# A hybrid attention/recurrence block on one core: PSUM as two allocations of four adjacent banks, a block's four sums added by one instruction, the second norm's factor applied once

## The chip, the cores and the metric

The kernel runs on one core of one Trainium2 chip. The metric is device time in microseconds (us) of one execution, from its start to its end; lower is better. Engines are named as in the profile: PE is TensorE (matmul), PEld its weight loads, DVE is VectorE, ACT is ScalarE, POOL is GpSimd, SP issues most of the DMAs.

## The reference, cut to what matters

One decoder layer over 256 positions of 2048 features, all in float32:

```python
a    = rmsnorm(h, norm_mix_pre)
proj = a @ w_in                       # 2048 x 17408: q, k, v of 3 attention groups, 4 parts of the recurrence, 2 gates
...                                   # rotary, three dilated windows of attention, merged by softmax denominators
...                                   # HGRN2 gated linear recurrence, per-head norm, output gate
y    = sigmoid(gate_a) * (attn @ w_attn_branch) + sigmoid(gate_r) * (r_out @ w_hgrn_branch)
h    = h + rmsnorm(y @ w_mix_out, norm_mix_post)
a    = rmsnorm(h, norm_ffn_pre)
gt, up = split(a @ w_ffn_gate_up)     # 2048 x (5632 + 5632)
ff   = (silu(gt) * up) @ w_ffn_down   # 5632 x 2048
h    = h + rmsnorm(ff, norm_ffn_post)
```

## The kernel before, in words

Every weight matrix is streamed once. `load` brings a piece of 512 KB into a `raw` buffer (SP's queue); `split` or `split_wide` makes of it a high part (ACT, a copy to the reduced-precision type fp32r) and a low part (DVE, the difference); `multiply` or `multiply_wide` then issues three products per tile (high by high, high by low, low by high) on PE, by the helper `mm` (L135). Work is a list of *blocks*, each of some *steps*. The order on every engine is the order in which the Python program issues instructions (`manual_schedule`); the split of a step stands two steps ahead of its matmuls (`AHEAD = 2`).

There are three kinds of block:

- **W blocks** (32 of them, four steps each): 256 columns of the weights are the stationary operand's columns, so results come out transposed, in two banks of PSUM. They make the recurrence's and the attention's projections. When one is done, `both_halves` evacuates it: for each of the two banks ACT copies one half (L237), then DVE adds the other half to it (L239).
- **N blocks** (12): 512 columns, two banks, one for each half of the positions. The two branch products, the output gate of the recurrence and the first piece of the feed-forward network's gate and up products are such blocks.
- **Wide blocks** (22, class `Wide`): 1024 columns, four result banks, keyed (side, group). Some of their steps save a product by a seven-product scheme, which needs four more banks, "p1", "p5", "p6" and "p7"; `gather` combines these into four pieces of SBUF (`b.rest`) after the last such step, and the block's evacuation (`evac_kept`, `evac_mix`, `evac_ffn`, `evac_down`) adds each result bank to its piece, bank by bank (for the feed-forward network L1327).

PSUM has eight banks of 2 KB per partition. Before, each bank is a tile of its own, drawn from two pools of four: `acc_bank()` and `aux()`. N and W blocks take two `acc` banks each, so two blocks alternate between two pairs. Wide blocks put their four results in one pool and the products "p1" to "p7" in the other, and swap (`flip`). Small work (transposes, attention, recurrence) takes `aux` banks; `turn_act` (L1295 and L1296) transposes a feed-forward result into two banks, which ACT copies out; `turn_side` (in the passage from the first half of the layer to the second) takes `acc` banks.

The evacuation of a block is a generator in the queue `evacs`. The main loop advances it by one `yield` after the matmuls of each step, so that the reads of a finished W or N block are issued **after** the matmuls of the next block's first step, which write the other pair of banks. Small work stands in the queues `lanes` and `turns`, advanced in the same place.

Of the kernel before, what the change touches and what calls it, by code (L numbers as in the profile page):

```python
# [19 lines left out]
P = 128  # L20
# [73 lines left out]
def tile_hybrid_block(ctx: ExitStack, tc: tile.TileContext, t, out):  # L94
# [7 lines left out]
    accp = ctx.enter_context(tc.tile_pool(name="accp", bufs=4, space=PSUM))  # L102
    auxp = ctx.enter_context(tc.tile_pool(name="auxp", bufs=4, space=PSUM))
# [14 lines left out]

    def aux():
# [8 lines left out]
    def eslot(s="e"):  # L128
        return p3(s, F32, 512, 6, "e")
# [103 lines left out]
    def both_halves(ev, i):  # L233
        def go(banks):
            s = ptile("sum").rearrange("p (h t) -> p h t", h=2)
            for n, ps in enumerate(banks):
                nc.scalar.activation(s[:, n, :], ps[:, S:], AF.Copy)  # L237
            for n, ps in enumerate(banks):
                nc.vector.tensor_add(s[:, n, :], ps[:, :S], s[:, n, :])  # L239
            yield from ev(i, s)  # L240
        return go
# [117 lines left out]

    def multiply_wide(st, sides=(0, 1), groups=(0, 1)):  # L360
        b, i = st.block, st.i
        m, by7 = b.order[i]

        def bank(key):

            if key not in b.bank:
                b.bank[key] = aux() if b.flip == (type(key) is not tuple) else acc_bank()
            return b.bank[key]

        def prod(key, x, w, j, last=False):  # L370
            ps = bank(key)
# [24 lines left out]
        prod((1, 1), act_of(1, 1), t, 3)  # L396

    def gather(b):

        e = {k: p3("e", F32, 512, 6) for k in ((0, 1), (1, 1), (0, 0), (1, 0))}  # L400
        x = b.bank
        nc.scalar.activation(e[0, 1], x["p1"], AF.Copy)
        nc.vector.tensor_add(e[1, 1], x["p6"], e[0, 1])
        nc.vector.tensor_add(e[0, 0], x["p5"], e[1, 1])
# [34 lines left out]
    class Split:  # L439
# [41 lines left out]
        def turned(self, src, n0, n):  # L481

            for i in range(n):
                ps = aux()
                for kk in range(2):
                    for b in range(2):
                        at = kk * S + b * P
                        c = (2 * i + kk) * P
                        nc.tensor.transpose(ps[:, at : at + P], src[:, b, c : c + P], ident)  # L489
                yield  # L490
                self.put(n0 + i, ps.rearrange("p (k t) -> p k t", k=2))

    def transpose_in(src, gcol, dst, c, apart=False):

        ps = []
        for k in (2 * c, 2 * c + 1):
            if apart or not ps:
                bank = aux()
            ps.append(bank[:, :S] if apart else bank[:, (k % 2) * S : (k % 2 + 1) * S])
# [10 lines left out]
        def low(kk):  # L510
            k = 2 * c + kk
            nc.vector.scalar_tensor_tensor(
                out=dst(k)[1], in0=ps[kk], scalar=gcol[:, k : k + 1],
                in1=dst.f32(k), op0=OP.mult, op1=OP.subtract,
            )

        if apart:
            return high, low
        high(0), high(1), low(0), low(1)

    def row_broadcast(dst, rc):
# [9 lines left out]
        nc.scalar.activation(dst, ps[:, :S], AF.Copy)  # L531

# [56 lines left out]
    def opening():  # L589
# [14 lines left out]
        nc.vector.tensor_copy(colg[:, 16:48], ps[:, :32])  # L604
        l0, l1 = colg[:, 32:40], colg[:, 40:48]
# [23 lines left out]
    def keep_warm(n):  # L629

        ps = aux()
        for _ in range(n):
            mm(ps, warm[:, :P], warm, True, True)

    def start():
# [3 lines left out]
        nc.vector.tensor_copy(colg[:, :16], ps[:, :16])  # L639
        high, low = transpose_in(xt, colg, xT, 0, True)  # L640
# [29 lines left out]
    def evac_kept(key, fn):  # L670
        def go(b):
            dst, at = keep(key, 1024), [(0, 0), (0, 1), (1, 0), (1, 1)]
            for k in at:
                nc.vector.tensor_add(b.rest[k], b.bank[k], b.rest[k])
            for s, g in at:
                e = b.rest[s, g]
                nc.scalar.activation(e, e, fn, scale=r1c[:, s : s + 1])
                nc.gpsimd.dma_start(dst[:, s, g * 512 : (g + 1) * 512], e)
                if (s, g) == (0, 1):
                    yield  # L680
            yield
# [64 lines left out]
    def evac_g(half):  # L746
        def go(banks):
# [4 lines left out]
            for i, ps in enumerate(banks):  # L752
                nc.scalar.activation(s[i], ps, AF.Sigmoid, scale=r1c[:, i : i + 1])
                nc.scalar.activation(dst[:, i, :], ps, AF.Copy, scale=r1c[:, i : i + 1])
            for _ in range(1 if half == 0 else 4):
                yield
# [46 lines left out]
    def attention(pair, hh):  # L803
# [4 lines left out]
        for par in range(2):  # L808
# [15 lines left out]
            nc.scalar.activation(p, p, AF.Exp, scale=-1.0, bias=m[:, 0:1], accum_out=m[:, 1:2])  # L824
            yield
# [10 lines left out]
            nc.scalar.activation(pt, ps, AF.Copy)  # L836
            yield
# [9 lines left out]
        nc.vector.tensor_sub(lo, o[:, :S], attnT[0].f32(head))  # L847
        done.append(head)
# [3 lines left out]
    def recurrence(half):  # L852
# [28 lines left out]
        def over_features(x, place):  # L881
# [5 lines left out]
            def go():  # L887
# [10 lines left out]
                for ps, there in zip(banks, place):  # L898
                    yield
                    there(ps)  # L900

# [40 lines left out]
        def products(lev, w):  # L942

            ps = aux()
            if w < 64:
# [7 lines left out]
                put(lev, w)(ps)  # L953
            elif w == 64:
# [7 lines left out]
                )  # L962
            else:
# [5 lines left out]
                nc.scalar.activation(a2[0], ps, AF.Copy)  # L969

# [48 lines left out]
        for i in range(2):  # L1019
            for h in range(4):  # L1020
# [4 lines left out]
                )  # L1025
            yield
        yield
        for j in range(2):
# [7 lines left out]
            recT[0].put(2 * half + j, ps.rearrange("p (h t) -> p h t", h=2), True)  # L1036
            if j == 1:
# [8 lines left out]
    def evac_rec_branch(j):  # L1046
        def go(banks):
            part[j] = hslot("part")
            for i in range(2):
                nc.vector.tensor_mul(part[j][:, i, :], banks[i], gates["r", j][:, i, :])  # L1050
                yield
        return go

    def evac_attn_branch(j):
        def go(banks):
# [3 lines left out]
            for i in range(2):  # L1059
                nc.vector.tensor_mul(g[:, i, :], banks[i], g[:, i, :])  # L1060
            yield
# [42 lines left out]
    def mix_sum(j, i, b):  # L1104
        e = b.rest[i, j % 2]
        nc.vector.tensor_add(e, b.bank[i, j % 2], e)

    def mix_square(j, i, b):
        sq = zss[0][:, 4 * i + j : 4 * i + j + 1]
        nc.scalar.activation(ptile("junk"), b.rest[i, j % 2], AF.Square, accum_out=sq)  # L1110

    def mix_gain(j, i, b):
        if j not in zg:
            zg[j] = sided(rslot("zg"))
        nc.vector.tensor_mul(
            zg[j][:, i, :], b.rest[i, j % 2],
# [3 lines left out]
    def evac_mix(b):  # L1120
        at = [(j, i) for i in range(2) for j in range(2)]
        for j, i in at:
            mix_sum(j, i, b)
# [28 lines left out]
    def turn_side(c, i):  # L1152
# [12 lines left out]
        def low():  # L1165
            for k, x in at:
# [3 lines left out]
                )  # L1170
        return high, low
# [114 lines left out]
    def turn_act(u, b):  # L1286
# [3 lines left out]
        for i in range(2):  # L1290
# [7 lines left out]
            )  # L1298

    def evac_first_gate(banks):  # L1300
        g = gate_t[0] = [eslot("g") for _ in range(2)]
        src = banks
        if "r2" not in ready:
            for i in range(2):
                nc.scalar.activation(g[i], banks[i], AF.Copy)
                yield
            src = g
            while "r2" not in ready:
                yield
        for i in range(2):  # L1310
            nc.scalar.activation(g[i], src[i], AF.Silu, scale=r2c[:, i : i + 1])
            yield

    def evac_first_up(banks):
        u = [eslot("u") for _ in range(2)]
        for i in range(2):
            nc.vector.scalar_tensor_tensor(
                out=u[i], in0=banks[i], scalar=r2c[:, i : i + 1], in1=gate_t[0][i],
                op0=OP.mult, op1=OP.mult,
            )  # L1320
        turns.append(u)
        yield

    def evac_ffn(b):
        e, x = b.rest, b.bank
        for key in ((0, 0), (0, 1), (1, 0), (1, 1)):
            nc.vector.tensor_add(e[key], x[key], e[key])  # L1327
            s, g = key
            if g == 0:
                nc.scalar.activation(e[key], e[key], AF.Silu, scale=r2c[:, s : s + 1])  # L1330
        yield
        for s in range(2):
            nc.vector.scalar_tensor_tensor(
                out=e[s, 1], in0=e[s, 1], scalar=r2c[:, s : s + 1], in1=e[s, 0],
                op0=OP.mult, op1=OP.mult,
            )
        turns.append([e[0, 1], e[1, 1]])
# [33 lines left out]
    def down_sum(j, i, b):  # L1371

        f = b.rest[i, j % 2]
        nc.vector.tensor_add(f, b.bank[i, j % 2], f)  # L1374

    def down_square(j, i, b):
        sq, r2 = fss[0][:, 4 * i + j : 4 * i + j + 1], r2c[:, i : i + 1]
        nc.scalar.activation(ptile("junk"), b.rest[i, j % 2], AF.Square, scale=r2, accum_out=sq)  # L1378

    def down_gain(j, i, b):  # L1380
        if i == 0:
            fz[j] = p3("fz", F32, 1024, 4, "so").rearrange("p (b c) -> p b c", b=2)
        nc.vector.scalar_tensor_tensor(
            out=fz[j][:, i, :], in0=b.rest[i, j % 2], scalar=r2c[:, i : i + 1],
# [4 lines left out]
    def evac_down(b):  # L1389
        parts = [(j, i) for i in range(2) for j in range(2)]  # L1390
        for j, i in parts:
            down_sum(j, i, b)
# [224 lines left out]
```

## Time and profile before

| | |
|---|---|
| median of 3 timed runs | 1701.61 us (1701.57 to 1703.21) |
| the profiled execution, first to last instruction | 1699.6 us |
| PE busy | 1689.1 us, 99% |
| DVE busy | 1423.5 us, 84% |
| ACT busy | 908.5 us, 53% |
| POOL busy | 40.5 us, 2% |
| granted TensorE clock, mean | 0.998 |

The profiled execution is one run beside the timed ones; its span is 2.0 us under their median, which is what lies before the first and after the last instruction and the difference from run to run. A group row of the profile reads: line, engine, operation, tiles out and in, shapes, how often, then busy us and mean ns of one. A timeline row reads: start us, us, engine, line, operation, tiles, how often. In the last column of either stands the idle time before it and who ended it. Line numbers of the profile are those of the kernel before; in the changed kernel `mm` is L157, the two reads of a W block are L259 and L261, and `turn_act` is L1347 and L1348.

### The profile page before, as it was taken

How to read it: one execution, taken by the hardware profiler on the slowest of the kernel's cores; microseconds unless marked ns; L12 is line 12 of the kernel's file. 1: busy time of each engine (PE TensorE's matmuls, PEld its weight loads, DVE VectorE, ACT ScalarE, POOL GpSimd, SP SyncE). 2: the span in 40 equal slices, each digit the busy share in tenths (PEclk: the TensorE clock that was granted, in tenths of full speed). 3: DMA queues.
4: the chain of work that ended last, by engine and by line, in shares of the span. 5: the costliest groups of instructions: out<-in, count | busy, mean ns of one | idle time of the engine just before them, and what ended most of it. 6: DMA issues, size and time to landing. Idle time of an engine off the chain costs nothing.

```text
span 1699.6 us, 21507 instructions
## 1 busy us (share of the span) xinstructions
PE 1689.1 (99%) x8265; PEld 1420.0 (84%) x8265; DVE 1423.5 (84%) x1604; ACT 908.5 (53%) x1023; POOL 40.5 (2%) x72
## 2 busy tenths in 40 slices
PE   9999999999999999999999999999999999999997
PEld 7888888888888888888888888888888888888886
DVE  6998888886887987776668889888888888898988
ACT  6655555554535434544445575555555555565663
POOL 0000000001000000000000000000000000000000
PEclk9999999999999999999999999999999999999999
DMA  8666666667546555565457646555555555656653
GB/s 288 220 231 232 232 232 233 228 229 258 180 149 196 188 174 175 173 216 168 154 179 249 237 147 223 198 198 198 198 198 198 198 198 198 221 195 212 200 198 114
DMA packets 206614, 344.77 MB, mean 203 GB/s; under 512 B 10960, under 2 KB 77568, under 8 KB 206512
## 3 DMA queue, kind: packets, MB, share of 16 engines
q1 hardware_dynamic: 198208, 317.89, 55.7%
q0 software_dynamic: 5680, 19.60, 3.3%
q10 hardware_dynamic: 2624, 5.92, 1.0%
q8 instruction: 64, 1.05, 0.2%
q14 instruction: 38, 0.31, 0.1%
HBM read 331.83 MB, written 11.53 MB: 202 GB/s over the span
## 4 chain that ended last, share of the span: by engine, by line
PE 98%; DVE 1%; ACT 0%; issue 0%; DVEq 0%; ACTq 0%
PE acc L135 61%; PE aux L135 35%; PE aux L833 0%; PE aux L501 0%; PE acc L1295 0%; DVE fz L1422 0%; PE aux L1295 0%; PE aux L489 0%; ACT junk L1378 0%; DVE e L1374 0%; DVE w L302 0%; DVE wl L338 0%; PE aux L1033 0%; PE acc L1158 0%; DVE g L758 0%
## 5 line engine op out<-in xcount | busy, mean ns | idle before, releaser
L338 DVE TENSOR_TENSOR wl<-raw,w 128x2048 fp32r<-128x2048 f32 x134 | 306.8, 2289 | 92.3 <-ACT w L336 90.9
L135 PE MATMUL acc<-xT,w 128*128 128x256 f32 (+1 forms) x2048 | 369.8, 339 | 0.0
L135 PEld LDWEIGHTS acc<-xT,w 128*128 128x128 f32 x2048 | 312.0, 188 | 43.8
L302 DVE TENSOR_TENSOR w<-raw,w 128x1024 fp32r<-128x1024 f32 (+1 forms) x191 | 232.5, 1218 | 136.0 <-ACT w L301 135.1
L336 ACT ACTIVATE w<-raw 128x2048 fp32r<-128x2048 f32 x134 | 256.1, 1911 | 149.3 <-PE aux L135 62.6
L301 ACT ACTIVATE w<-raw 128x1024 fp32r<-128x1024 f32 (+1 forms) x191 | 200.9, 1053 | 230.2 <-PE acc L135 187.8
L135 PE MATMUL acc<-w,hT 128*128 128x512 f32 x598 | 175.5, 390 | 0.0
L347 ACT ACTIVATE w<-sum 128x1024 fp32r<-128x1024 f32 x70 | 74.4, 1063 | 186.5 <-DVE sum L342 186.5
L355 DVE TENSOR_TENSOR wl<-sum,w 128x1024 fp32r<-128x1024 f32 (+1 forms) x128 | 168.8, 1321 | 0.0
L135 PE MATMUL acc<-w,xT 128*128 128x512 f32 x536 | 155.1, 392 | 0.0
L135 PE MATMUL aux<-w,hT 128*128 128x512 f32 x430 | 135.7, 389 | 0.0
L135 PEld LDWEIGHTS acc<-w,hT 128*128 128x128 f32 x598 | 111.7, 188 | 23.2 <-DVE w L302 0.2
L357 DVE TENSOR_TENSOR dl<-raw,dh 128x1536 fp32r<-128x1536 f32 x70 | 123.0, 1758 | 8.8 <-ACT dh L353 7.2
L135 PEld LDWEIGHTS acc<-w,xT 128*128 128x128 f32 x536 | 99.9, 188 | 20.9 <-DVE w L302 0.3
L135 PE MATMUL aux<-w,xT 128*128 128x512 f32 x344 | 108.5, 389 | 0.0
L353 ACT ACTIVATE dh<-raw 128x1536 fp32r<-128x1536 f32 x70 | 103.1, 1473 | 0.0
L135 PEld LDWEIGHTS aux<-w,hT 128*128 128x128 f32 x430 | 80.7, 188 | 16.8
L135 PE MATMUL acc<-wl,hT 128*128 128x512 f32 x227 | 86.9, 390 | 0.0
L350 ACT ACTIVATE w<-sum 128x1024 fp32r<-128x1024 f32 x70 | 74.4, 1062 | 21.8 <-DVE sum L349 21.8
L342 DVE TENSOR_TENSOR sum<-raw 128x1024 f32<-128x1024 f32 x70 | 85.2, 1217 | 0.0
L135 PE MATMUL aux<-wl,hT 128*128 128x512 f32 x215 | 83.6, 389 | 0.0
L135 PE MATMUL aux<-w,a 128*128 128x512 f32 x268 | 83.6, 389 | 0.0
(293 smaller groups left out, 2776.8 us busy)
## 6 DMA issues: line engine op xcount, KB each, us to landing
raw<-in_w_in SPq DMA_DIRECT2D x271, 512.0 KB, 4.6
raw<-in_w_ffn_gate_up SPq DMA_DIRECT2D x176, 512.0 KB, 4.4
raw<-in_w_ffn_down SPq DMA_DIRECT2D x88, 512.0 KB, 4.8
raw<-in_w_mix_out SPq DMA_DIRECT2D x32, 512.0 KB, 5.3
kept<-e POOLq DMA_DIRECT2D x32, 256.0 KB, 4.2
raw<-in_w_hgrn_branch SPq DMA_DIRECT2D x16, 512.0 KB, 4.9
raw<-in_w_attn_branch SPq DMA_DIRECT2D x16, 512.0 KB, 4.5
v<-kept POOLq DMA_DIRECT2D x8, 512.0 KB, 5.7
```

What stands on the lines that cost most here:

```text
L135: nc.tensor.matmul(ps, lhsT, rhs, start=start, stop=stop, skip_group_check=True)
L301: nc.scalar.activation(wh[:, k], raw[:, k], AF.Copy)
L302: nc.vector.tensor_sub(wl[:, k], raw[:, k], wh[:, k].bitcast(F32))
L336: nc.scalar.activation(hi, raw, AF.Copy)
L338: nc.vector.tensor_sub(lo, raw, hi.bitcast(F32))
L342: nc.vector.tensor_sub(s[:, :1024].rearrange("p (a c) -> p a c", a=2), raw[:, 512:1536].rearrange("p (a c) -> p a c", a=2), raw[:, None, : ...
L347: nc.scalar.activation(hi[:, :1024], s[:, :1024], AF.Copy)
L350: nc.scalar.activation(hi[:, 1024:], s[:, 1024:], AF.Copy)
L353: nc.scalar.activation(dhi, d, AF.Copy)
L355: nc.vector.tensor_sub(lo[:, x], s[:, x], hi[:, x].bitcast(F32))
L357: nc.vector.tensor_sub(dlo, d, dhi.bitcast(F32))
```

## The change

1. PSUM is now two tiles, `acc` and `aux`, of four adjacent banks each, which live from the beginning to the end. `bank_of` hands out a view of one bank from a list of idle ones and `free` gives it back; both are bookkeeping in Python and issue nothing.
2. A wide block takes its four result banks at once, in order (`all_four`), so that `add_up` adds all four banks to the four pieces by one DVE instruction of 128x2048. The four pieces are one tile (`four_e`) with one buffer instead of six small ones.
3. `gather`'s last two additions, which both add "p7", are one instruction.
4. In the feed-forward network the second norm's factor `r2c` was applied to the gate and to the up product, and again after the down product; now it is left out at the up product, and the two products per block are one instruction of 128x1024.
5. The kept results are written by two DMAs of 512 KB per block instead of four of 256 KB.

```diff
-    accp = ctx.enter_context(tc.tile_pool(name="accp", bufs=4, space=PSUM))
-    auxp = ctx.enter_context(tc.tile_pool(name="auxp", bufs=4, space=PSUM))
+    psum = ctx.enter_context(tc.tile_pool(name="psum", bufs=1, space=PSUM))
...
+    fours = {n: psum.tile([P, 4, 512], F32, name=n) for n in ("acc", "aux")}
+    idle = {n: deque(range(4)) for n in fours}
+    held = {}
+    def bank_of(n):
+        i = idle[n].popleft()
+        ps = fours[n][:, i, :]
+        held[id(ps)] = (n, i, ps)
+        return ps
...
     def aux():
-        return auxp.tile([P, 512], F32, tag="aux", name=nm("aux"))
+        return bank_of("aux")
     def acc_bank():
-        return accp.tile([P, 512], F32, tag="acc", name=nm("acc"))
+        return bank_of("acc")
...
-        nc.vector.tensor_add(e[1, 0], x["p7"], e[0, 0])
-        nc.vector.tensor_add(e[1, 1], x["p7"], e[1, 1])
+        nc.vector.tensor_add(
+            e[:, 2:], x["p7"][:, None, :].to_broadcast([P, 2, 512]), e[:, 0:4:3]
+        )
...
+    def add_up(b):
+        nc.vector.tensor_add(b.rest, out_of(b), b.rest)
+        free_out(b)
...
     def evac_ffn(b):
-        for key in ((0, 0), (0, 1), (1, 0), (1, 1)):
-            nc.vector.tensor_add(e[key], x[key], e[key])
...
-            nc.vector.scalar_tensor_tensor(
-                out=e[s, 1], in0=e[s, 1], scalar=r2c[:, s : s + 1], in1=e[s, 0],
-                op0=OP.mult, op1=OP.mult,
-            )
+        add_up(b)
...
+        nc.vector.tensor_mul(e[:, 1:4:2], e[:, 1:4:2], e[:, 0:4:2])
```

The instructions on PE stay, 8031 matmuls in nearly the same order. What each waits for moves. A row below is a line, an instruction with its tiles, its shape, and in brackets the engines' semaphores that it waits for.

**PE, at the border of the first two W blocks**, the end of the second block's first step and the beginning of its second step (`xT` is the activations, `w` the split weights). Before:

```order
L135 MATMUL acc_3128<-xT_113,w_3081 128x512
L135 MATMUL acc_3128<-xT_113,w_3081 128x256 x2
L135 MATMUL acc_3128<-xT_113,w_3081 128x512
L135 MATMUL acc_3127<-xT_114,w_3102 128x512 [waits Activation_49]
L135 MATMUL acc_3127<-xT_114,w_3102 128x256 [waits DVE_49]
L135 MATMUL acc_3127<-xT_114,w_3102 128x256
```

Of the change, at the same place:

```order
L157 MATMUL acc<-xT_112,w_2908 128x512
L157 MATMUL acc<-xT_112,w_2908 128x256 x2
L157 MATMUL acc<-xT_112,w_2908 128x512
L157 MATMUL acc<-xT_113,w_2929 128x512 [waits DVE_49,Activation_49]
L157 MATMUL acc<-xT_113,w_2929 128x256 x2
```

Before, the second step's first matmul waits for ACT's high part of its weights and the second for DVE's low part. In the change the first also waits for DVE, and the counts in the built program are those of the second DVE add (L261) and the second ACT copy (L259) of the *first* block, which read the other pair of banks.

**ACT, at the same border**: the splits of the steps ahead, and between them the two copies out of the first block's banks. Before:

```order
L301 ACTIVATE w_3102<-raw_2911 128x1024 [waits DMAHW0_49,DVE_49,PE_49]
L301 ACTIVATE w_3122<-raw_2941 128x1024 [waits DMAHW1_49,DVE_49,PE_49]
L237 ACTIVATE sum_3145<-acc_3043 128x256
L237 ACTIVATE sum_3145<-acc_3044 128x256
L301 ACTIVATE w_3152<-raw_2941 128x1024 [waits DMAHW2_49,DVE_49,PE_49]
```

Of the change:

```order
L324 ACTIVATE w_2929<-raw_2751 128x1024 [waits DMAHW0_49,DVE_49,PE_49]
L324 ACTIVATE w_2949<-raw_2781 128x1024 [waits DMAHW1_49,DVE_49,PE_49]
L259 ACTIVATE sum_2970<-acc 128x256 [waits PE_49]
L259 ACTIVATE sum_2970<-acc 128x256
L324 ACTIVATE w_2977<-raw_2781 128x1024 [waits DMAHW2_49,DVE_49]
```

The order is the same; the copy now waits for PE, and its count in the built program is that of the last matmul of the second block's first step, which writes a bank that the copy does not read.

**PE, at `turn_act` of the first wide block of the feed-forward network**: two banks, four transposes each. Before:

```order
L135 MATMUL aux_8589<-w_8528,hT_8009 128x512
L1295 MATMUL acc_8628<-ident,u_8547 128x128 [waits DVE_49]
L1295 MATMUL acc_8628<-ident,u_8548 128x128 [waits DVE_49]
L1295 MATMUL acc_8628<-ident,u_8547 128x128
L1295 MATMUL acc_8628<-ident,u_8548 128x128
L1295 MATMUL acc_8634<-ident,u_8547 128x128
```

Of the change:

```order
L157 MATMUL aux<-w_8157,hT_7654 128x512
L1347 MATMUL acc<-ident,e_8033 128x128 [waits DVE_49]
L1347 MATMUL acc<-ident,e_8033 128x128 x3
L1347 MATMUL acc<-ident,e_8033 128x128 [waits Activation_49]
L1347 MATMUL acc<-ident,e_8033 128x128 x3
L157 MATMUL aux<-dh_8186,hT_7650 128x512
```

The fifth transpose, into the second bank, now waits for ACT, by its count for the copy out of the first bank; before it waited for nothing.

More of the change, by code (lines that the diff above doesn't have):

```diff
@@ L117, in hslot, with free, all_four, four_e @@
         return hpool.tile([P, 2, 512], F32, tag="h", bufs=4, name=nm(s))
+    fours = {n: psum.tile([P, 4, 512], F32, name=n) for n in ("acc", "aux")}
[6 more added lines that the diff above has]
+        return ps
+    def free(*banks):
+        for ps in banks:
+            n, i, _ = held.pop(id(ps))
+            idle[n].append(i)
+    def all_four(n):
+        assert len(idle[n]) == 4
+        idle[n] = deque(range(4))
+        return [bank_of(n) for _ in range(4)]
     def aux():
-        return auxp.tile([P, 512], F32, tag="aux", name=nm("aux"))
+        return bank_of("aux")
     def acc_bank():
-        return accp.tile([P, 512], F32, tag="acc", name=nm("acc"))
+        return bank_of("acc")
     def p3(s, dtype, n, bufs, tag=None):
         return pool["now"].tile([P, n], dtype, tag=tag or s, bufs=bufs, name=nm(s))
-    def eslot(s="e"):
-        return p3(s, F32, 512, 6, "e")
+    def four_e():
+        return p3("e", F32, 2048, 1).rearrange("p (n c) -> p n c", n=4)
     def small(s, n=8, bufs=6):
@@ L239, in go @@
                 nc.vector.tensor_add(s[:, n, :], ps[:, :S], s[:, n, :])
+            free(*banks)
             yield from ev(i, s)
@@ L358, in split_wide, with out_of @@
         st.parts = hi, lo, dhi, dlo
+    def out_of(b):
+        return fours["acc" if b.flip else "aux"]
     def multiply_wide(st, sides=(0, 1), groups=(0, 1)):
@@ L362, in multiply_wide, with prod @@
         m, by7 = b.order[i]
-        def bank(key):
+        if not b.bank:
+            b.bank = dict(zip(((0, 0), (0, 1), (1, 0), (1, 1)), all_four("acc" if b.flip else "aux")))
+        def prod(key, x, w, j, last=False):
             if key not in b.bank:
[L367 to L371, printed above, removed]
+                b.bank[key] = aux() if b.flip else acc_bank()
+            ps = b.bank[key]
             wh, wl = (v[:, j * 512 : (j + 1) * 512] for v in w)
@@ L491, in turned @@
                 self.put(n0 + i, ps.rearrange("p (k t) -> p k t", k=2))
+                free(ps)
     def transpose_in(src, gcol, dst, c, apart=False):
-        ps = []
+        ps, banks = [], []
         for k in (2 * c, 2 * c + 1):
@@ L498, in transpose_in @@
                 bank = aux()
+                banks.append(bank)
             ps.append(bank[:, :S] if apart else bank[:, (k % 2) * S : (k % 2 + 1) * S])
@@ L515, in low @@
             )
+            if apart:
+                free(banks[kk])
         if apart:
@@ L519, in transpose_in @@
         high(0), high(1), low(0), low(1)
+        free(*banks)
     def row_broadcast(dst, rc):
@@ L531, in row_broadcast @@
         nc.scalar.activation(dst, ps[:, :S], AF.Copy)
+        free(ps)
     def by_side(x):
@@ L633, in keep_warm @@
             mm(ps, warm[:, :P], warm, True, True)
+        free(ps)
     def start():
@@ L671, in go @@
         def go(b):
[L672 to L676, printed above, removed]
+            dst = keep(key, 1024)
+            add_up(b)
+            for s in range(2):
+                e = b.rest[:, 2 * s : 2 * s + 2].rearrange("p g c -> p (g c)")
                 nc.scalar.activation(e, e, fn, scale=r1c[:, s : s + 1])
[L678 to L681, printed above, removed]
+                nc.gpsimd.dma_start(dst[:, s, :], e)
+                yield
         return go
@@ L836, in attention @@
             nc.scalar.activation(pt, ps, AF.Copy)
+            free(ps)
             yield
@@ L900, in go @@
                     there(ps)
+                    free(ps)
             behind.append(go())
@@ L953, in products @@
                 put(lev, w)(ps)
+                free(ps)
             elif w == 64:
@@ L962, in products @@
                 )
+                free(ps)
             else:
@@ L1025, in recurrence @@
                 )
+            free(o[i])
             yield
@@ L1050, in go @@
                 nc.vector.tensor_mul(part[j][:, i, :], banks[i], gates["r", j][:, i, :])
+                free(banks[i])
                 yield
@@ L1060, in go @@
                 nc.vector.tensor_mul(g[:, i, :], banks[i], g[:, i, :])
+            free(*banks)
             yield
@@ L1170, in low @@
                 )
+            free(ps)
         return high, low
@@ L1298, in turn_act @@
             )
+            free(ps)
     def evac_first_gate(banks):
-        g = gate_t[0] = [eslot("g") for _ in range(2)]
+        e = gate_t[0] = four_e()
         src = banks
@@ L1383, in down_gain @@
         nc.vector.scalar_tensor_tensor(
-            out=fz[j][:, i, :], in0=b.rest[i, j % 2], scalar=r2c[:, i : i + 1],
+            out=fz[j][:, i, :], in0=b.rest[:, 2 * i + j % 2], scalar=r2c[:, i : i + 1],
             in1=fpost[j // 2][:, (j % 2) * 512 : (j % 2 + 1) * 512],
```

73 lines of the change are left out of this document (42 added, 31 removed).

## The prediction

> **What bounds the kernel now.** I read the page first, then who waits for whom on PE, then the chain.
>
> ```profile
> span 1699.6 us, 21507 instructions
> PE 1689.1 (99%) x8265; PEld 1420.0 (84%) x8265; DVE 1423.5 (84%) x1604; ACT 908.5 (53%) x1023; POOL 40.5 (2%) x72
> ```
>
> The page cannot say whether 99% is a full engine or one that crawls; the waits of PE's own rows can:
>
> ```profile
> PE aux L135 <- DVE warm L159: 1.2, 1, 1.2
> PE aux L135 <- DVE wl L338: 0.6, 1, 0.6
> ```
>
> These two are all its waits, 1.8 us of 1699.6. In the chain that ended last, a stretch of a wide block reads:
>
> ```profile
> 97.94 12.24 PE acc L135 x54
> ```
>
> 12.24 us over 54 is 0.227 us from one 512-column matmul to the next, and wide blocks keep this pace throughout. So PE is the bound, with no slack to give: its 8031 matmuls stay, so what DVE or ACT save is worth nothing, and every wait that the change puts on PE is added to the time whole. The question is only which waits there are and how long.
>
> **What the saved work is worth.** The border of two feed-forward blocks shows the evacuation that becomes one instruction, from the timeline:
>
> ```profile
> 1074.26 2.28 DVE L338 TENSOR_TENSOR wl<-raw,w 128x2048 fp32r<-128x2048 f32 x1
> 1076.45 2.48 DVE L1327 TENSOR_TENSOR e<-aux,e 128x512 f32<-128x512 f32 x4
> 1085.70 1.41 DVE L1333 SCALAR_TENSOR_TENSOR e<-e,r2c,e 128x512 f32<-128x512 f32 x2
> 1077.03 0.39 PE L135 MATMUL aux<-w,hT 128*128 128x512 f32 x1
> 1088.14 1.03 PE L1295 MATMUL aux<-ident,e 128*128 128x128 f32 x8
> ```
>
> ```profile
> L1327 DVE TENSOR_TENSOR e<-aux,e 128x512 f32<-128x512 f32 x20 | 12.4, 682 | 0.0
> L348 DVE TENSOR_TENSOR sum<-raw,sum 128x512 f32<-128x512 f32 x70 | 48.4, 692 | 2.4
> kept<-e POOLq DMA_DIRECT2D x32, 256.0 KB, 4.2
> ```
>
> Four adds take 2.48; one of 128x2048 has no row with a PSUM operand, and I take the 2.28 of L338, since L1327, which reads PSUM, takes 682 ns where L348 with all in SBUF takes 692. That saves 0.2 on DVE in 20 blocks, some 4 us; the merged last two additions of the gather and the merged products save less than 0.2 a block each. All of it lies beside PE and counts zero. It also has a price: the single add cannot begin before the last matmul into the fourth bank ends (1077.03 + 0.39 = 1077.42), so it ends near 1079.7 instead of 1078.93, 0.8 later. The products then end near 1087.9 instead of 1087.11, and PE takes them up at 1088.14. The cover shrinks from 1.0 to 0.2 us and I cost this at nothing; if it is gone, ten blocks lose a few tenths each, under 5 us. The single `four_e` buffer is rewritten by the gather some 30 us later, when the DMAs (4.2 us to landing on the page) and transposes that read it are long done; the two DMAs for four run on POOL's queue with the same bytes. Both count zero.
>
> **What the two allocations add.** The rows of order in the section on the change show it: with all four banks in one tile that is never released, a matmul into one bank is held until the reads of *any other* bank of this tile, issued before it, are done, and a read until the matmuls into any other bank, issued before it, are done. Before, those were different tiles. The border of two W blocks is where this bites most. In the timeline of before:
>
> ```profile
> 399.75 6.43 PE L135 MATMUL acc<-xT,w 128*128 128x512 f32 x36
> 400.45 0.64 ACT L237 ACTIVATE sum<-acc 128x256 f32<-128x256 f32 x2
> 401.72 0.75 DVE L239 TENSOR_TENSOR sum<-acc,sum 128x256 f32<-128x256 f32 x2
> ```
>
> PE runs on without a break while ACT and then DVE read the old pair. In the change the chain is serial: PE finishes the next block's first step, then ACT copies, then DVE adds, and only then may PE begin the second step. Nothing hides this, however early ACT and DVE are free, since ACT's copy must wait for PE and PE for DVE's add. DVE's following split stands behind its adds and ACT's behind its copies, but both are two steps ahead of PE and the halt is PE's too.
>
> The price of one hand-off comes from the only halt of PE in mid-stream:
>
> ```profile
> 54.01 2.29 DVE L338 TENSOR_TENSOR wl<-raw,w 128x2048 fp32r<-128x2048 f32 x1
> 56.35 0.50 PE L135 MATMUL aux<-wl,xT 128*128 128x512 f32 x1 [0.56 <-DVE wl L338]
> 56.69 0.64 PE L135 MATMUL aux<-w,xT 128*128 128x512 f32 x2
> 57.86 0.39 PE L135 MATMUL aux<-wl,xT 128*128 128x512 f32 x1
> ```
>
> DVE ends at 56.30 and PE starts at 56.35: 0.05 per hand-off. The next matmul starts 0.34 later instead of 0.227: 0.11 for starting again. A matmul in mid-stream lasts 0.39 and the next could start after 0.227, so a reader that waits for its end costs 0.16. With one reading engine the fixed part is 0.16 + 2 x 0.05 + 0.11 = 0.37, with two in succession 0.42.
>
> *W blocks.* 0.42 + 0.64 + 0.75 = 1.81 us at a border. There are 32 W blocks, hence 31 borders, the last of them towards the first N block: 56 us if nothing covers them. At 12 of them small matmuls of the attention or the recurrence stand between the two steps in the order, mostly four, of which this timeline row shows the size (each counts as two records):
>
> ```profile
> 619.91 1.11 PE L135 MATMUL aux<-pt,v 128*128 128x128 f32 x8
> ```
>
> That would cover about 0.9 each, 11 us, leaving 45; on the other side ACT and DVE are late at some borders with the attention's and recurrence's own work. I take **50**, bounds 42 and 65.
>
> The other places are read off the groups, one row each (the last two rows are of the timeline):
>
> ```profile
> L1050 DVE TENSOR_TENSOR part<-acc,gate 128x512 f32<-128x512 f32 x8 | 5.5, 684 | 0.0
> L1060 DVE TENSOR_TENSOR gate<-acc,gate 128x512 f32<-128x512 f32 x8 | 5.1, 683 | 0.0
> L1296 ACT ACTIVATE act<-acc 128x512 f32<-128x512 f32 x12 | 6.5, 596 | 14.5 <-PE acc L1295 14.5
> L1374 DVE TENSOR_TENSOR e<-acc,e 128x512 f32<-128x512 f32 x4 | 2.8, 688 | 1.7 <-PE acc L135 1.7
> L753 ACT ACTIVATE sig<-acc,r1c 128x512 f32<-128x512 f32 x4 | 2.7, 684 | 0.0
> L916 DVE COPY_PREDICATED at<-lmask,aux 128x512 f32<-128x512 int32 x13 | 12.4, 950 | 0.1
> L302 DVE TENSOR_TENSOR w<-raw,w 128x1024 fp32r<-128x1024 f32 x189 | 231.2, 1224 | 136.0 <-ACT w L301 135.1
> 988.02 0.63 ACT L1163 ACTIVATE hT<-acc,colg 128x128 fp32r<-128x128 f32 x2 [0.38 <-PE acc L1158]
> 988.84 0.60 DVE L1167 SCALAR_TENSOR_TENSOR hT<-acc,colg,hT 128x128 fp32r<-128x128 f32 x2
> ```
>
> - *Branch products* (8 N blocks): the first four are read a bank per step, 8 waits of 0.37 + 0.68; the other four both banks at once, 4 waits of 0.37 + 1.29 (two in succession: 0.68 and, as in the four adds above, 0.61): **15**.
> - *`turn_act`* (11 times): the second bank's transposes wait for the copy of the first, 0.37 + 0.60 = 0.97: **11**.
> - *`turn_side`* (6 times): two copies and two differences, 0.42 + 0.63 + 0.60: **10**.
> - *The last block of the mix and the last of all*, whose sums are taken bank by bank between their matmuls: six waits of 0.37 + 0.69: **6**.
> - *Recurrence and attention* in `aux`: some 30 waits for a read of another bank; most of those reads are a step old (2.8 us, a quarter of a W block) when PE arrives. For about six I count DVE's 0.95 with a split of 1.22 (L302's group mean) ahead of it, 2.3 each: **14**; bounds 0 and 40, the nearest row being L916.
> - *The two output-gate and the first feed-forward blocks, the start and the first W block*: reads of two banks by ACT (0.68 each, up to four in a row), the opening's transposes behind DVE's reads, and the one 2.28 add that stands before the first W block: 4 + 4 + 4 + 3 = **15**.
>
> The sum is 50 + 15 + 11 + 10 + 6 + 14 + 15 = 121 us. The profiled span of 1699.6 would become 1821, and the median, 2.0 above its span, **1823 us**.
>
> **The rivals.** *The clock falls in the halts.* The windows at the end show the granted clock (after the busy times of PE, PEld, DVE, ACT and POOL), and the timeline the pace at the start:
>
> ```profile
> 1690.50:1693.00 2.50, 0.37 (x2) 0.00 (x0) 2.00 (x6) 1.30 (x4) 0.00 (x0) 1.00 0.03 11
> 1693.00:1699.50 6.50, 0.00 (x0) 0.00 (x0) 3.25 (x7) 0.01 (x1) 0.00 (x0) 0.51 0.45 161
> 1.20 3.59 PE L135 MATMUL aux<-warm 128*128 128x512 bf16 x8 [1.20 <-DVE warm L159]
> 7.29 1.86 PE L135 MATMUL acc<-w,xT 128*128 128x512 f32 x6
> ```
>
> PE ends 0.37 into the first window, at 1690.87, and the clock is halved at about 1693.1: 2.2 us of idleness sufficed there. Eight matmuls in 3.59 us are 0.43 apiece, and the faster pace comes near 7 us, 5.8 after the first; a fall therefore costs some 5.8 x (1 - 0.227/0.43) = 2.7 us. Halts of 1.8 are shorter than the idleness shown and those over 2.2 are perhaps ten: 27 us, **1850**. Falls at the W borders too would make it 40 or so, 108 us more, **1931**. The Trainium skill (TensorE: Matmul & The Clock Gate, Part 1) says that the clock halves after at least one idle window of about 3.4 us and that the windows run freely; by this rule no halt of 1.8 us would bring it down, and the sum stays near 1823. Here it fell sooner, 2.2 us after the last matmul, so that a window need not be idle from end to end. I give 15% to falls at the long halts alone and 7% to falls at most borders.
>
> *The waits are there and cost nothing*: the counts they name were passed when PE arrives, as in before, where nearly every matmul of a step waits for weights long ready. Then PE is as full as now, and the time is **1701.6**, within 0.2%, about what a measurement of this kernel can tell. The point from which it decides is whether a copy can start before the next step's matmuls end. Against it stand the counts in the built program, for the copy and the resumed step alike, which form a closed chain. For it speaks only that I read those counts and did not see them run: 4%. The Trainium skill (PSUM, on bank collisions) says that engines may work in different banks at the same time; the rows at 399.75 agree. By it the chip needs none of these waits, and the sum would be zero; but the program's semaphores hold PE whether the chip needs it or not.
>
> *Only the closed chains bind*: W borders, `turn_act` and `turn_side` as priced, half of the W borders covered by small matmuls, the rest hidden: 28 + 11 + 10 + 15 = 64, **1766**. 12%.
>
> **How the numbers follow.** The forecast of 1823 has 62%; its own range is 1800 to 1848, from the bounds of the W borders (-8, +15) and of the recurrence (-14, +10 where more than six bind). To leave out no more than two in ten the range reaches to the falls at long halts, 1868 with the W borders' upper bound, and down to 1780, part of the way to the third rival. Faster by over 0.2% is 1%: nothing takes matmuls from PE. Within 0.2%: 3%. Slower: 96%.
>
> **What would show it.** In the profile after, PE's waits must name DVE L261 some 27 to 31 times with about 1.5 us idle each, ACT L1348 eleven times with near 0.9, and DVE L1099, L1110 and L1218; ACT's L259 must wait for PE. DVE's busy time should fall by 5 to 10 us to no effect. The granted clock should stay at 1.0 in the middle. It would be wrong if PE's waits stay under 10 us, or if the clock shows 0.5 inside the W stage.

## The result and the profile after

| | before | after |
|---|---|---|
| median | 1701.61 us (1701.57 to 1703.21) | 1831.47 us (1831.38 to 1835.17) |
| ratio, 95% interval | | 1.0767 (1.0752 to 1.0782) |
| profiled span | 1699.6 us | 1829.6 us |
| mean granted clock | 0.998 | 0.991 |

The change costs 7.7%. The forecast was 1823 with a range of 1780 to 1868. The page of after, in the same rows as that of before:

```profile
span 1829.6 us, 21375 instructions
PE 1720.6 (94%) x8265; PEld 1429.9 (78%) x8265; DVE 1424.5 (78%) x1512; ACT 906.9 (50%) x1007; POOL 31.6 (2%) x56
```

PE has the same number of records, but its idle time grew from 1699.6 - 1689.1 = 10.5 us to 109.0. DVE, whose instructions were merged, is as busy as before. Who PE waits for (total us, times, longest), the largest rows of 28:

```profile
PE acc L157 <- ACT w L324: 17.4, 12, 1.7
PE acc L157 <- DVE sum L261: 16.1, 10, 3.0
PE acc L157 <- DVE m L867: 8.6, 5, 3.0
PE acc L157 <- DVE hT L1218: 5.8, 4, 1.5
PE aux L157 <- DVE at L949: 4.9, 2, 3.1
PE acc L157 <- DVE gate L1110: 4.4, 3, 1.5
PE acc L1347 <- ACT act L1348: 4.1, 6, 0.7
PE acc L157 <- ACT e L1365: 3.9, 2, 3.1
PE acc L157 <- DVE part L1099: 3.5, 4, 0.9
PE aux L1347 <- ACT act L1348: 3.4, 5, 0.7
```

Before, this view had two rows and 1.8 us. Now the timeline of one W border:

```profile
404.75 6.67 PE L157 MATMUL acc<-xT,w 128*128 128x512 f32 x37
411.45 0.66 ACT L259 ACTIVATE sum<-acc 128x256 f32<-128x256 f32 x2 [1.73 <-PE acc L157]
412.00 1.06 ACT L324 ACTIVATE w<-raw 128x1024 fp32r<-128x1024 f32 x1
412.14 0.76 DVE L261 TENSOR_TENSOR sum<-acc,sum 128x256 f32<-128x256 f32 x2 [1.16 <-ACT sum L259]
413.05 7.23 PE L157 MATMUL acc<-xT,w 128*128 128x512 f32 x40 [1.63 <-ACT w L324]
```

PE's step ends at 411.42, ACT copies from 411.45 to 412.11, DVE adds from 412.14 to 412.90, and PE goes on at 413.05. Before, the same copies and adds ran while PE multiplied. The profile puts this halt down to ACT's L324, a split for a later step that ended at 413.06, when PE had already begun; the add ended at 412.90. By the counts in the built program it is the add that PE waits for, and the name in the row is only that of the event that came last. The start and end times settle it: at the 26 borders between W blocks where PE halts, and at the last one, towards the branch products, PE begins 0.145 or 0.146 us after the end of the second add, whatever name the wait has, while the nearest split of L324 ends anywhere from 0.58 us before PE's start to 2.74 us after it. So the borders must be summed over all names, from the group of these matmuls:

```profile
L157 PE MATMUL acc<-xT,w 128*128 128x512 f32 x1024 | 344.1, 406 | 43.4 <-ACT w L324 16.7 <-DVE sum L261 16.1 <-DVE m L867 6.6
```

Where the 130.0 us lie shows in the first and last start of a tile's matmuls (after the count: shortest, median and longest ns), first of before, then of after:

```profile
L135 PE MATMUL acc<-xT,w x2048: 274/337/497, 388.1 to 801.9; 128*128 128x512 f32 x94, 128*128 128x256 f32 x93
L135 PE MATMUL acc<-w,recT x192: 387/389/476, 802.2 to 852.7; 128*128 128x512 f32 x192
```

```profile
L157 PE MATMUL acc<-xT,w x2048: 274/393/774, 397.2 to 881.7; 128*128 128x512 f32 x94, 128*128 128x256 f32 x93
L157 PE MATMUL acc<-w,recT x192: 387/389/632, 882.0 to 941.0; 128*128 128x512 f32 x192
```

The W stage took 802.2 - 388.1 = 414.1 us before and 882.0 - 397.2 = 484.8 after. The other stages are cut in the same way at the first starts of the tiles yT, hT and a. The two columns on the right are worked out from the start times of all 8265 matmul records of after: how many halts of PE end in the stage or at its end, with what they add to the usual spacing (the halt, with the drain before it and the slower restart behind it), and the longer spacing of matmuls that begin while the clock is halved.

| stage | before | after | more | halts | half clock |
|---|---|---|---|---|---|
| start, to the first W block | 388.1 | 397.2 | 9.1 | 5, 9.1 | 1.6 |
| W blocks, with attention and recurrence | 414.1 | 484.8 | 70.7 | 32, 62.2 | 9.0 |
| branch products | 99.7 | 117.6 | 17.9 | 11, 16.0 | 1.6 |
| mix | 85.8 | 92.4 | 6.6 | 4, 5.0 | 1.4 |
| feed-forward, gate and up | 470.9 | 492.1 | 21.2 | 17, 21.3 | 0 |
| down | 241.0 | 245.5 | 4.5 | 4, 4.3 | 0 |
| sum | 1699.6 | 1829.6 | 130.0 | 73, 117.9 | 13.6 |

Halts and half clock make 131.5 us; before had one halt too, of 0.8 us with drain and restart, so that 130.7 stand against the 130.0 measured.

### The profile page after: what moved, and what is told of

Same layout as the page of the kernel before. It is cut to its first block, busy times and chain, and to the rows that moved or that the text cites. A ratio compares the mean times of both kernels' runs of the same rounds, so it can differ in the third digit from the quotient of the medians.

```text
span 1829.6 us, 21375 instructions
## 1 busy us (share of the span) xinstructions
PE 1720.6 (94%) x8265; PEld 1429.9 (78%) x8265; DVE 1424.5 (78%) x1512; ACT 906.9 (50%) x1007; POOL 31.6 (2%) x56
## 4 chain that ended last, share of the span: by engine, by line
PE 57%; DVE 2%; ACT 2%; issue 1%; DVEq 0%; ACTq 0%
PE acc L157 34%; PE aux L157 22%; ACT w L324 1%; DVE w L325 0%; DVE sum L261 0%; ACT act L1348 0%; PE acc L1347 0%; PE aux L1347 0%; PE aux L874 0%; DVE fz L1472 0%; PE aux L522 0%; DVE part L1099 0%; ACT sum L259 0%; ACT hT L1214 0%; DVE gate L1110 0%
## 5 line engine op out<-in xcount | busy, mean ns | idle before, releaser
L157 PE MATMUL acc<-xT,w 128*128 128x256 f32 (+1 forms) x2048 | 381.6, 344 | 43.4 <-ACT w L324 16.7
L157 PEld LDWEIGHTS acc<-xT,w 128*128 128x128 f32 x2048 | 318.2, 192 | 94.9 <-ACT sum L259 23.4
L361 DVE TENSOR_TENSOR wl<-raw,w 128x2048 fp32r<-128x2048 f32 x134 | 306.8, 2289 | 92.6 <-ACT w L359 90.9
L324 ACT ACTIVATE w<-raw 128x1024 fp32r<-128x1024 f32 (+1 forms) x191 | 201.1, 1053 | 226.4 <-PE acc L157 176.7
L157 PE MATMUL acc<-w,a 128*128 128x512 f32 x268 | 84.6, 390 | 2.6 <-DVE e L1422 2.6
```

The source lines that it names most:

```text
L157: nc.tensor.matmul(ps, lhsT, rhs, start=start, stop=stop, skip_group_check=True)
L324: nc.scalar.activation(wh[:, k], raw[:, k], AF.Copy)
L361: nc.vector.tensor_sub(lo, raw, hi.bitcast(F32))
```

## The experiments

Each is compared with the kernel before on the same chip; the ratio's 95% interval is in brackets.

### Eight tiles of one bank each

The whole change stays, but for the allocation and the add, which must then be four.

```diff
-    fours = {n: psum.tile([P, 4, 512], F32, name=n) for n in ("acc", "aux")}
+    group = {'acc': 1, 'aux': 1}
+    fours = {
+        n: [psum.tile([P, k, 512], F32, name=f"{n}{i}") for i in range(4 // k)]
+        for n, k in group.items()
+    }
...
-        nc.vector.tensor_add(b.rest, out_of(b), b.rest)
+        n = "acc" if b.flip else "aux"
+        for i, ps in enumerate(fours[n]):
+            e = b.rest[:, i * group[n] : (i + 1) * group[n]]
+            nc.vector.tensor_add(e, ps, e)
```

> The change with each of the eight banks as a tile of its own again, and therefore four adds per block for one; the rest of the change stays (one buffer for the four pieces, the gather's merged addition, the merged products, the factor once, two DMAs for four). If the waits between banks of one allocation are the whole cause: 1701.6 within 2 us, and PE idle under 15 us. If the merged instructions, the longer wait for the last bank or the single buffer hold PE: above 1710, with PE waiting for DVE at the transposes of the feed-forward results.

Measured: 1701.54 us, 0.9997 (0.9988 to 1.0007). The page:

```profile
PE 1688.8 (99%) x8265; PEld 1419.6 (84%) x8265; DVE 1419.6 (84%) x1572; ACT 906.0 (53%) x1007; POOL 31.9 (2%) x56
```

All waits of PE:

```profile
PE aux L161 <- DVE warm L185: 1.2, 1, 1.2
PE aux L161 <- DVE wl L365: 0.6, 1, 0.6
PE acc L161 <- DVE w L329: 0.2, 1, 0.2
```

All of the loss is gone with the two allocations, though the merged gather, the merged products, the missing factor, the single buffer of pieces and the larger DMAs are still there. DVE's 3.9 us less (1419.6 for 1423.5) and ACT's 2.5 less (906.0 for 908.5) bought nothing.

### The two allocations alone

First the kernel before with only the allocation changed. In this kernel banks are handed out in turn without the list of idle ones, so that one can be handed out while its last holder is still unread. What it returns is therefore not the layer's result, and it is read for its time alone.

```diff
...
+    fours = {n: psum.tile([P, 4, 512], F32, name=n) for n in ("acc", "aux")}
+    turn = {"acc": 0, "aux": 0}
+    def bank_of(n):
+        i = turn[n] % 4
+        turn[n] += 1
+        return fours[n][:, i, :]
...
```

> The kernel before with one part of the change alone: the two allocations of four banks, handed out in turn, with all adds bank by bank and all else as before. If the waits between banks are the whole cause: 1831 within 5 us. If the merged instructions share in it: well under, by their share; if they do it alone: 1702.

Measured: 1833.87 us, 1.0774 (1.0758 to 1.0790). Then the same question from the other side: the changed kernel with its list of idle banks, its merged instructions undone (four adds, two gather additions, two products per block).

```diff
...
-        nc.vector.tensor_add(b.rest, out_of(b), b.rest)
+        for i in range(4):
+            e = b.rest[:, i]
+            nc.vector.tensor_add(e, out_of(b)[:, i], e)
...
-        nc.vector.tensor_mul(e[:, 1:4:2], e[:, 1:4:2], e[:, 0:4:2])
+        for k in (0, 2):
+            nc.vector.scalar_tensor_tensor(
+                out=e[:, k + 1], in0=e[:, k + 1], scalar=1.0, in1=e[:, k],
+                op0=OP.mult, op1=OP.mult,
+            )
```

> The changed kernel with its merged instructions undone: four adds of one bank each for the single add, two last additions in the gather for one, two products per feed-forward block for one; the two allocations, the views of idle banks and the single buffer of four pieces stay. If the allocations alone are the cause: the change's 1831 within 4 us. If merging helps or hurts by more than can be measured: 1815 or less, or 1845 or more.

Measured: 1834.07 us, 1.0779 (1.0761 to 1.0797), the same as after within both intervals. The allocations alone make the whole loss. The group of the W blocks' matmuls is that of after:

```profile
L157 PE MATMUL acc<-xT,w 128*128 128x256 f32 (+1 forms) x2048 | 381.9, 344 | 43.6 <-ACT w L324 17.1 <-DVE sum L261 15.7 <-DVE m L868 6.5
```

### How the loss divides between acc and aux

Three kernels differ only in how many banks share a tile, and so in how many adds a wide block takes. The edit is that of the first experiment with other sizes:

```diff
+    group = {'acc': 2, 'aux': 4}  # pairs of acc
+    group = {'acc': 4, 'aux': 1}  # single aux
+    group = {'acc': 1, 'aux': 4}  # single acc
```

Pairs of `acc`: the two banks of a W block share a tile, its neighbour's two are another.

> The change with the four acc banks as two allocations of two, so that a block's pair and the next block's are different tiles again; aux stays one allocation, sums in acc by two instructions. If the terms of the prediction have the right sizes: the W borders (50) and the branch products (15) go, with parts of the passage to the second half and the last block; some 45 are left: 1745 within 8. If the waits at the W borders are covered or are not the large term: above 1780. No wait of PE for the add of a W block should be left.

Measured: 1753.58 us, 1.0304 (1.0289 to 1.0320). The group of the W blocks' matmuls:

```profile
L161 PE MATMUL acc<-xT,w 128*128 128x256 f32 (+1 forms) x2048 | 371.3, 340 | 0.0
```

The largest waits left:

```profile
PE acc L161 <- DVE hT L1223: 4.3, 2, 2.3
PE aux L1352 <- ACT act L1353: 3.4, 5, 0.7
PE acc L1352 <- ACT act L1353: 3.4, 5, 0.7
```

43.4 us of idle time at these matmuls became 0.0 with one number changed: the waits came from reads of *other* banks of the tile. The passage between the halves (`hT`) and `turn_act`, which read one bank of a pair while PE wants the other, still wait. The expected 1745 within 8 was missed by 0.6 us: the halts that are left come to 44 us with drain and restart, for the 45 expected, but five spells at half clock, which the sum did not have, add 8.

> The change with the four aux banks as tiles of their own, acc one allocation. By the terms of the prediction recurrence and attention (14), five of eleven turn_act (5), half of the bank-by-bank sums (3) and most of the opening (4) go: 26 less, 1805 within 8. If the half-clock spells at 484, 634 to 655 and 767 us come from the long halts of the recurrence, they go with them, some 10 us more: 1795. If the aux waits are covered by the W borders' halts behind them: 1825 or more.

Measured with single `aux`: 1803.97 us, 1.0597 (1.0580 to 1.0615), the 1805 that the terms gave.

> The changed kernel with the four acc banks as tiles of their own, aux one allocation: the mirror of the run with aux apart, which left 102 of 130 us. If the halts simply add: 130 - 102 = 28, hence 1730 within 6. If halts on the one side cover halts on the other: more than 28, 1740 or above. By the terms of the prediction (aux: recurrence 14, turn_act 5, sums 3, opening 4): 1728.

Measured with single `acc`: 1734.6 us, 1.0193 (1.0178 to 1.0208). Against the before of the same chip, `acc` alone costs 1803.97 - 1701.84 = 102 us and `aux` alone 1734.6 - 1701.78 = 33 us, together 135 for 130 of both. The two are nearly additive, and three quarters lie in `acc`. The other idea for the single `aux`, that the clock would stay up and the time come to 1795, was not borne out. The spells of after at 484 and at 634 to 655 us were gone, but those at 767, 935 and 1000 stayed at the same matmuls, and three came at new places.

### The chain at the W border, made longer

If PE waits for ACT's copies in series, twice the copies must cost time, and in the kernel before, where they run beside PE, none. The same edit was made in both:

```diff
-                nc.scalar.activation(s[:, n, :], ps[:, S:], AF.Copy)
+                for _ in range(2):
+                    nc.scalar.activation(s[:, n, :], ps[:, S:], AF.Copy)
```

> The kernel before with the same two copies issued twice. If PE waits for no read of another pair of banks there: 1702 within 2. If even before the reads of a W block stood in PE's way: up to 17 us more.

Measured in before: 1701.79 us, 1.0001 (0.9992 to 1.0011). PE's only waits are again two, of 1.2 and 0.5 us.

> The changed kernel with each of the two ACT copies out of a W block's banks issued twice, two more copies of 256 columns per border; the result stays the same. If copies and adds form a closed chain with PE at the W borders: 0.27 us (the pace of such copies) x 2 x 31 = 17 us more, 1848 within 5. If ACT's reads are hidden behind PE's work at most borders: 1831 to 1836.

Measured in after: 1870.2 us, 1.0983 (1.0960 to 1.1006), 38.7 more than after. The timeline of the same border:

```profile
412.62 1.49 ACT L260 ACTIVATE sum<-acc 128x256 f32<-128x256 f32 x4 [1.73 <-PE acc L157]
414.14 0.76 DVE L262 TENSOR_TENSOR sum<-acc,sum 128x256 f32<-128x256 f32 x2 [1.99 <-ACT sum L260]
415.04 12.93 PE L157 MATMUL acc<-xT,w 128*128 128x512 f32 x64 [2.46 <-ACT w L325]
```

The chain is shown: the halt grew from 1.63 to 2.46, by the 0.83 that ACT's copies grew (1.49 for 0.66). The size is twice what was expected, for two reasons. Four copies take 1.49, more than twice 0.66; with that the halts come to 140.1 us with drain and restart, 22.2 more than in after. The rest is the clock: 18 spells at half clock instead of 7, whose longer spacing costs 27.8 us instead of 13.6. Together these are 36.4 of the 36.5 us by which the profiled spans differ (1866.1 and 1829.6). The windows of this border and of the two after it (busy us of PE, PEld, DVE, ACT, POOL, then the granted clock):

```profile
411.70:415.10 3.40, 0.94 (x6) 0.58 (x4) 1.37 (x4) 2.37 (x5) 1.14 (x2) 1.00 1.04 374
415.10:418.50 3.40, 3.40 (x11) 2.92 (x12) 1.66 (x2) 0.63 (x1) 0.00 (x0) 0.50 0.99 313
418.50:421.90 3.40, 3.40 (x22) 2.97 (x21) 1.15 (x2) 1.06 (x1) 0.00 (x0) 1.00 0.83 285
```

After a halt of 2.46 us PE does 11 matmuls in 3.4 us, and then 22.

## Why the prediction was right, step by step

**The mechanism** was right and is shown, not only argued: PE had no slack; dependencies kept for a whole tile made PE wait for reads of other banks; splitting the tiles removes the waits (1701.54), joining them alone makes them (1834.07), and the single instructions are worth nothing.

**The W border.** The forecast priced one at 1.81 us with drain and restart. Measured are 1.63 us of idle time, and 0.16 + 0.11 on top, 1.90. It is a little dearer because PE resumed 0.15 after DVE's end instead of 0.05. Of the group's 43.4 us, 2.5 stand ahead of the first W block. The other 41.0 are 26 borders: sixteen of 1.63 to 1.68 us, seven of 0.75 to 1.20, which small matmuls cover in part, and three of 1.82 to 3.04, where DVE or ACT came late. With 0.27 each they make 48 us for the forecast's 50. The forecast named 27 to 31 waits for L261; by this name there are ten, and the rest stand under L324, L867 and L932. The wait itself was there at 27 borders, these 26 and the last (0.74 us idle), for 1.54 us in the mean.

**The W stage as a whole** was forecast at 50 + 14 = 64 and its halts measure 62.2. It grew by 70.7, and the 9.0 us at half clock are the difference. The 14 for recurrence and attention, six waits of 2.3 us, had bounds of 0 and 40. Six halts came, of 1.41 to 3.25 us of idle time, some 14 us in all. A count and a sum that fit so well out of such bounds are in part luck, and whether each halt is a read that stands behind a split was not followed.

**The other terms.** Branch products 15, measured halts 16.0 in that stage, of which two at its end (1.73 and 0.63 us idle) belong to no term. Gate and up with `turn_act`, `turn_side` and the first block's reads some 24, measured 21.3 and, at the end of the mix, 1.8 for one more halt of `turn_side`. The mix 3, measured 3.2 without that halt. Down 4, measured 4.3. The start some 11 (output gate, opening, the add before the first W block), measured 9.1. `turn_act`, in the timeline:

```profile
1203.53 1.22 DVE L1384 TENSOR_TENSOR e<-e 128x1024 f32<-128x1024 f32 x1
1205.15 0.60 PE L1347 MATMUL aux<-ident,e 128*128 128x128 f32 x4
1205.79 0.60 ACT L1348 ACTIVATE act<-aux 128x512 f32<-128x512 f32 x1 [2.16 <-PE aux L1347]
1206.43 0.66 PE L1347 MATMUL aux<-ident,e 128*128 128x128 f32 x4 [0.69 <-ACT act L1348]
```

Eleven waits came, as forecast. Each shows 0.69 idle where 0.9 was named, since 0.97 with drain and restart was the price and 0.69 + 0.27 = 0.96 is what it was. The products (L1384) end at 1204.75 and PE takes them up at 1205.15: the cover of the evacuation shrank from 1.0 to 0.4 and held, as costed.

**DVE** was to fall by 5 to 10 us. The single add takes 2292 ns (2.28 was assumed), and the two kernels that differ in the merges alone give the fall: 1430.1 us busy with the merges undone, 1424.5 with them, 5.6 less. But the allocations had raised DVE's busy time from 1423.5 to 1430.1, so against before nothing is left. These 6.6 lie in no row: the durations of all DVE instructions add up to 1495.6 us in both kernels. Busy time counts once what two neighbours overlap, and that is 72.1 us in before and 65.5 with the allocations.

**The clock** is where the forecast failed. It expected the clock at 1.0 in the middle and named as a sign of being wrong a clock of 0.5 inside the W stage. Four of the seven spells lie there, at 484, 634, 648 and 768 us. It gave falls at long halts 15%, at 2.7 us apiece. They came, seven spells of 3.4 or 6.8 us, 13.6 us in all, but not by the condition that it had, a halt longer than the 2.2 us of idleness at the end of before. Three spells followed shorter halts (1.81 us; 2.00; 1.73 and 0.63 in one window), and none followed four of the seven halts over 2.4 us (those that end at 48.53, 397.24, 748.68 and 1130.66). What decides is the idle time within one window of a fixed grid, as the last section shows; these four halts were cut in two by the grid.

Without the half clock the time would be near 1818. The halts came out 3 us lower than priced (117.9 for 121) and the clock 13.6 higher, so the one hid a little of the other, and that is luck. The measured time lies also in the forecast's own 1800 to 1848, but those bounds stood for dearer borders and a dearer recurrence, which did not come. The spells cost 13.6 us over nine windows, 1.5 us each and 1.9 a spell, not 2.7: the price had been taken from the start, where the slow pace lasted 5.8 us.

**The rivals.** "The waits cost nothing" fell with the result. "Only the closed chains" (1766) fell too: 27 of the 31 borders bind, not half of them, and `aux` costs 33 us of its own. "Falls at most W borders" (1931) did not come: an ordinary border of 1.63 us leaves the clock alone. It nearly came, though, since 0.83 us more per border brought 18 spells.

## What to carry to other kernels

Joining PSUM banks in one tile, so that one instruction can read them all, also joins their dependencies. Where PE is the bound and alternates between banks, look for the closed chain first, PE's next step, the old block's reads, PE again, and price it from a drain, the reads and the restart: here 1.9 us at an ordinary one of 26 borders, for merged instructions that were worth nothing because they ran beside a full PE. If a wide read is wanted, join only the banks that fill and drain together, and add the price of the clock where the idle time in one window passes half of it.

## What the runs showed of the hardware

**Half a window of idleness halves the clock.** Windows of after, an ordinary border and its successor, then the one that fell (480.80) with the two that follow:

```profile
436.40:439.80 3.40, 1.77 (x11) 1.34 (x10) 2.20 (x5) 1.68 (x4) 0.00 (x0) 1.00 0.74 255
439.80:443.20 3.40, 3.40 (x22) 2.96 (x21) 1.02 (x1) 1.53 (x2) 0.00 (x0) 1.00 0.32 84
480.80:484.20 3.40, 1.59 (x9) 1.17 (x8) 3.40 (x6) 2.12 (x2) 0.00 (x0) 1.00 0.11 14
484.20:487.60 3.40, 3.40 (x11) 2.80 (x11) 3.40 (x7) 0.00 (x0) 0.00 (x0) 0.50 0.87 296
487.60:491.00 3.40, 3.40 (x21) 2.95 (x21) 2.02 (x3) 1.06 (x1) 0.00 (x0) 1.00 0.00 0
```

PE was idle for 3.40 - 1.77 = 1.63 us of the first window and kept its clock, for 3.40 - 1.59 = 1.81 of the third and lost half of it in the next. In a run all spells begin at whole multiples of 3.4133 us from one another, the 18 of the kernel with doubled copies too, and last one such window or two. If the profiled executions of after and of the six experiments with halts are cut into these windows, counted from a run's first spell, no window at full clock with less than 1.80 us of idle time was followed by half clock, and all 57 with more than 1.92 us were (seven of them are the last of a run, where the matmuls end). Between lies a band that goes either way. The longest halt of after is 3.25 us, so no window between its first and last matmul was idle from end to end. The Trainium skill (TensorE: Matmul & The Clock Gate, Part 1) gives free-running windows of 3413 ns and a halved clock after at least one idle window. The length and the fixed grid agree with these runs; that the whole window must be idle does not, and the measurement decides: a little over half is enough.

**Four banks in one read.** One DVE add over four PSUM banks takes as long as one of this size in SBUF, 2292 and 2289 ns:

```profile
L439 DVE TENSOR_TENSOR e<-aux,e 128x2048 f32<-128x2048 f32 x10 | 22.9, 2292 | 6.7 <-PE aux L157 6.7
L361 DVE TENSOR_TENSOR wl<-raw,w 128x2048 fp32r<-128x2048 f32 x134 | 306.8, 2289 | 92.6 <-ACT w L359 90.9
```

Four adds in a row, which overlap a little, had taken 2.48. So the merge saves 0.2 us of DVE's time per block.
